# A hybrid encoder layer: one pair of work tiles kept at another address, and five small reorderings in its first stage

## The chip, the cores and the metric

The kernel runs on one core of one Trainium2 chip. The metric is the device time of one execution in microseconds (us). The engines are named as in the profile: PE is the matrix engine (PEld its weight loads), DVE the vector engine, ACT the scalar engine, POOL the engine that also takes small element-wise work, SP the queue from which most transfers are issued. Each engine works through its own instructions in a fixed order and waits on semaphores for the others.

## The reference, cut to what matters

Two sequences of 1024 rows by 1024 columns go through one encoder layer. The part that the change touches is the input side of the mixing sub-layer:

```
h = rmsnorm(x, g_mix) * (1.0 + sc1) + sh1          # sc1, sh1 from silu(c) @ w_ada
z = h @ w_in                                        # 256 + 128 + 64 + 512 columns
q_lat, kv_lat, k_pe, f_in = split(z)
y_mla  = attention(rmsnorm(q_lat), rmsnorm(kv_lat), rope(k_pe))
y_four = real(fft2(f_in over sequence and group columns)) @ w_four
mix = concat([y_mla, y_four]) @ w_out
x = x + ga1 * mix
```

Behind it stand a gated feed-forward layer (2816 wide) and a final norm. All results are float32.

## The kernel before

**Stages.** Stage 1 (from 0 to about 223 us) makes the latents and the Fourier inputs. Stage 2 (to about 300 us) does the transform along the sequence, multiplies it into the folded output weights and makes the second modulation. Stage 3 is attention (to about 680 us), and the feed-forward part fills the rest. Nearly every product is made of three matmuls on float32 operands that are split in a high and a low half: `split` writes the high half on ACT (line 62) and the low half on DVE (line 63), and `mm3` issues the three matmuls (lines 83 to 85).

**Stage 1** runs over eight pairs k = 0 to 7, four for each sequence. A pair is two blocks of 128 rows, j and j + 4, which the Fourier part adds and subtracts. For each pair there are these steps, and the steps of neighbouring pairs overlap:

- `norm_sq`: squares of the rows on ACT (line 377), then `rstd`, a chain of six small instructions on POOL (lines 107 to 114, from `rs_v` to `rs_r`). `norm_x`: the rows `xt` scaled by `rs_r` on DVE (line 389).
- `flip`: 16 transposes on PE (line 405) in two pairs of groups, g = 0, 1 and g = 2, 3, into PSUM banks; ACT and DVE read them out to `hf`, `hh` and `hl`.
- `zproj` / `z_mm`: the latent columns of z on PE. `z_out`: their squares on ACT (lines 462 and 463), `rstd` on POOL again (`rs_v<-mz`), the rotary key on DVE and POOL (lines 480 to 484) and the normalised latents `lat` on DVE (lines 486 and 487).
- `latents`: four transposes of `lat` for each of the two blocks on PE (line 501), split by ACT into `lh` and by DVE into `ll`, and two stores to `lat_d` in HBM.
- `evenodd`: sums and differences `eo` of the two blocks on POOL (line 428), split by ACT into `eoh` and by DVE into `eol`. There is one `eo` buffer.
- `fourier_in(k, 0)` and `fourier_in(k, 1)`: 24 matmuls each with 280 and 256 columns, called the cosine and the sine product below.

Between these steps a generator, `extras()`, is called for one step at a time by `next(more)`. It makes the modulation row (matmuls at line 219, transfers of `wada`), `fold_q` (eight matmuls at line 242, results taken out of PSUM by DVE at line 243), `fold_out` and last the folding of the output gate into `wm_d`: four matmuls at line 325 and four results `so` on DVE (line 330) for each step, which leave by stores to HBM. `so`, `lat` and the modulation row share three buffers (tag `sk`).

**What sets the order.** The program is written in one order and put into an order for each engine when it is built; `issue_after(x)`, `chained(f)` (behind the last named PE instruction) and `behind()` (behind the last split) constrain that order. On the chip the order of each engine is fixed, and an instruction that waits holds up all that stand behind it on its engine.

**Memory.** The tiles of stage 1 lie in a pool `p1`. Stage 2 opens pools over the same addresses, with waits for each tile: a tile of stage 2 may be written when the tiles of stage 1 that lay there are done with. In the kernel before, the two buffers each of `lh` and `ll` lie at bytes 91424 to 99616 of a partition, and three stage 2 tiles lie on them: the small `An` and `nyn`, `ny` (93984) and `A` (from 96032). `ny` is written by line 899, `A` by the first splits of stage 2.

## Time and profile before

| what | value |
|---|---|
| median of 3 runs | 2037.05 us (2036.78 to 2038.44) |
| the profiled execution: its own time / its span | 2039.17 us / 2037.4 us |
| mean granted PE clock | 0.993 |
| PE busy over the span | 1988.9 us, 98% |
| PE busy 0 to 223 us | 206.5 of 223 us |
| PE busy 223 to 300 us | 74.7 of 77 us |
| PE busy 300 to 680 us | 373.8 of 380 us |
| PE busy 680 to 2037 us | 1333.9 of 1357 us |

The profile shows one execution, which took 2.1 us more than the median of the runs; 1.77 us of its time lie outside the span. A timeline row reads: start, busy time (both in us), engine, line of the kernel, operation, result and operands, number of instructions, and in brackets the idle time of the engine ahead of the row with what ended it. The windows view gives for a stretch the busy time of each engine, then the clock granted to PE (1.00 is full speed, 0.50 half), then the share of the transfer engines that was busy.

### The profile page before, as it was taken

To read this page: it belongs to the slowest core of one execution; us is meant where nothing else is said; L and a number is where in the kernel's file an instruction comes from. 1 tells how busy PE (TensorE), PEld (TensorE's weight loads), DVE (VectorE), ACT (ScalarE), POOL (GpSimd) and SP (SyncE) were. 2 spreads that over 40 slices of the span, in tenths; PEclk is the share of its full clock that TensorE was granted. 3 is DMA by queue.
4 is the path that set the end of the run, shared out by engine and by line. 5 is a ranking of instruction groups with operands and counts; after the bars stand their busy time and mean duration, and the time that the engine had idled before them with its cause. 6 is when DMAs were issued, how large, how long until landed. Compare 5 with 4: busy or idle time off the path is not lost.

```text
span 2037.4 us, 28290 instructions
## 1 busy us (share of the span) xinstructions
PE 1988.9 (98%) x9840; PEld 1624.8 (80%) x9840; DVE 1415.8 (69%) x2088; ACT 896.8 (44%) x1733; POOL 828.6 (41%) x1013
## 2 busy tenths in 40 slices
PE   8899999999999999999999999999999999999997
PEld 7688777888777778888888888877788888888876
DVE  5676657766676679888677677677756655657674
ACT  4565545555555564333333365453333333336441
POOL 2454112111313227879779410333654454510142
PEclk9999999999999999999999999999999999999999
DMA  9685793445554475545645587674422322357662
GB/s 377 209 289 169 235 346 116 114 104 120 144 125 134 120 265 195 197 169 193 210 160 193 177 301 252 217 234 148 138 98 104 113 95 103 114 189 269 229 217 90
DMA packets 181963, 370.33 MB, mean 182 GB/s; under 512 B 18556, under 2 KB 58236, under 8 KB 177724
## 3 DMA queue, kind: packets, MB, share of 16 engines
q1 hardware_dynamic: 163148, 310.71, 45.5%
q0 software_dynamic: 18672, 57.81, 9.3%
q8 instruction: 77, 1.26, 0.3%
q14 instruction: 66, 0.54, 0.1%
HBM read 256.46 MB, written 120.39 MB: 185 GB/s over the span
## 4 chain that ended last, share of the span: by engine, by line
PE 54%; DVE 2%; DMA 2%; POOL 1%; issue 1%; ACT 1%; SPq 0%; DVEq 0%; ACTq 0%; POOLq 0%
PE bank L84 18%; PE bank L83 18%; PE bank L85 18%; DVE wl L63 1%; DMA val<-x_d 1%; DMA draw<-s_d 1%; DVE val L143 1%; POOL val L143 0%; ACT wh L62 0%; DVE val L1761 0%; DMA draw<-t_d 0%; POOL rs_y L110 0%; DVE val L1735 0%; DMA rgu<-in_wgu_dram 0%; DMA draw<-in_w_down_dram 0%
## 5 line engine op out<-in xcount | busy, mean ns | idle before, releaser
L83 PE MATMUL bank<-H,wh 128*128 128x512 f32 x1224 | 477.2, 390 | 6.4 <-DVE val L143 5.8
L85 PE MATMUL bank<-H,wl 128*128 128x512 f32 x1224 | 476.4, 389 | 0.2 <-DVE wl L63 0.2
L84 PE MATMUL bank<-H,wh 128*128 128x512 f32 x1224 | 476.2, 389 | 0.0
L143 DVE TENSOR_TENSOR val<-bank,val 128x512 f32<-128x512 f32 x244 | 166.7, 688 | 164.7 <-PE bank L85 163.5
L83 PEld LDWEIGHTS bank<-H,wh 128*128 128x128 f32 x1224 | 229.7, 188 | 56.9 <-DVE val L143 6.6
L85 PEld LDWEIGHTS bank<-H,wl 128*128 128x128 f32 x1224 | 229.7, 188 | 49.1 <-DVE wl L63 1.5
L84 PEld LDWEIGHTS bank<-H,wh 128*128 128x128 f32 x1224 | 229.7, 188 | 47.6
L63 DVE TENSOR_TENSOR wl<-draw,wh 128x512 fp32r<-128x512 f32 x286 | 201.6, 740 | 83.5 <-ACT wh L62 83.0
L62 ACT CAST wh<-draw 128x512 fp32r<-128x512 f32 x286 | 168.9, 621 | 158.9 <-PE bank L84 81.5
L84 PE MATMUL bank<-wl,wh 128*128 128x512 f32 x572 | 223.6, 391 | 3.5 <-DVE wl L63 3.5
L143 POOL TENSOR_TENSOR val<-val 128x512 f32<-128x512 f32 x58 | 82.7, 1434 | 347.4 <-DVE val L1735 192.4
L83 PE MATMUL bank<-wh 128*128 128x512 f32 x572 | 222.7, 389 | 0.4 <-ACT wh L62 0.4
L85 PE MATMUL bank<-wh,wl 128*128 128x512 f32 x572 | 222.6, 389 | 0.0
L62 ACT CAST wh<-rgu 128x512 fp32r<-128x512 f32 x171 | 106.5, 624 | 250.4 <-PE bank L84 194.1
L63 DVE TENSOR_TENSOR wl<-val,wh 128x512 fp32r<-128x512 f32 x133 | 142.9, 1076 | 70.6 <-ACT wh L62 70.5
L63 DVE TENSOR_TENSOR wl<-rgu,wh 128x512 fp32r<-128x512 f32 x171 | 166.7, 976 | 7.6 <-ACT wh L62 7.5
L62 ACT CAST wh<-val 128x512 fp32r<-128x512 f32 x133 | 82.4, 623 | 178.7 <-PE bank L84 158.3
L140 POOL TENSOR_TENSOR val<-rgu 128x512 f32<-128x512 f32 x80 | 114.1, 1426 | 99.7 <-DMA rgu<-in_wgu_dram 91.0
L84 PEld LDWEIGHTS bank<-wl,wh 128*128 128x128 f32 x572 | 107.3, 188 | 28.7 <-DVE wl L63 6.6
L83 PEld LDWEIGHTS bank<-wh 128*128 128x128 f32 x572 | 107.4, 188 | 23.2 <-ACT wh L62 0.8
L85 PEld LDWEIGHTS bank<-wh,wl 128*128 128x128 f32 x572 | 107.4, 188 | 22.1
L140 POOL TENSOR_TENSOR val<-val 128x512 f32<-128x512 f32 x89 | 119.3, 1357 | 1.3
(393 smaller groups left out, 3924.2 us busy)
## 6 DMA issues: line engine op xcount, KB each, us to landing
rgu<-in_wgu_dram SPq DMA_DIRECT2D x86, 512.0 KB, 4.9
draw<-s_d SPq DMA_DIRECT2D x143, 256.0 KB, 3.8
s_d<-val POOLq DMA_DIRECT2D x88, 256.0 KB, 3.9
draw<-t_d SPq DMA_DIRECT2D x88, 256.0 KB, 4.1
s_d<-val SPq DMA_DIRECT2D x66, 256.0 KB, 3.5
wada<-in_wa_dram SPq DMA_DIRECT2D x16, 1024.0 KB, 11.8
draw<-in_w_down_dram SPq DMA_DIRECT2D x55, 256.0 KB, 4.5
xt<-in_x_dram SPq DMA_DIRECT2D x16, 512.0 KB, 6.9
```

The source lines that it names most:

```text
L62: here["a"] = nc.scalar.copy(hi, src).ins
L63: here["v"] = nc.vector.tensor_tensor(out=lo, in0=src, in1=rd(hi), op=ALU.subtract).ins
L83: nc.tensor.matmul(out, lh, rh, start=first, stop=False, skip_group_check=cont)
L84: nc.tensor.matmul(out, lh, rl, start=False, stop=False, skip_group_check=cont)
L85: here["pe"] = nc.tensor.matmul(out, ll, rh, start=False, stop=last, skip_group_check=cont).ins
L140: return eng.tensor_tensor(out=out, in0=x, in1=y, op=ALU.subtract).ins
L143: return eng.tensor_tensor(out=out, in0=x, in1=y, op=ALU.add).ins
```

## The change

Five edits, all in stage 1:

1. Two dummy tiles for each of the tags `lh` and `ll` are taken right behind the Fourier weights of pool `p1`. A tag keeps its place, so `lh` and `ll` lie at bytes 83136 to 91328, and `ropec`, `ropes`, `c2`, `lw`, `zoc`, `vecs`, `scT` and `b1` move up by 8192 bytes. The stage 2 tiles `An`, `ny` and `A` stay where they are and now lie on some of these. No instruction is added.
2. `fold_q` issues both matmuls of a head, and then both DVE operations.
3. `z_out(0)` (the squares of pair 0's latents and what follows) is placed ahead of `norm_sq(2)`, which is held behind its last square.
4. In pairs 5 and 6 the first of the three `extras()` steps is left out at its place and called at the end of the pair.
5. In the last pair the latents of its second block are flipped behind the sine product; before, behind the cosine product.

```diff
--- before.py
+++ after.py
@@ -192,6 +192,9 @@
         wz_l = w.tile([P, NC, DZ], F32R, name="wz_l")
         wcs_f = [w.tile([P, NC * NCS + NZC - NCOS], F32R, name=f"wcs_{x}") for x in "hl"]
         wcs_h, wcs_l = [t[:, : NC * NCS].rearrange("p (c n) -> p c n", c=NC) for t in wcs_f]
+        for t in ("lh", "ll"):
+            for _ in range(2):
+                w.tile([P, 512], F32R, tag=t, name=t, bufs=2)
         ropec = w.tile([P, 8, ROPE], F32, name="ropec")
         ropes = w.tile([P, 8, ROPE], F32, name="ropes")
         c2 = w.tile([P, P], F32, tag="c2", name="c2")
@@ -240,6 +243,7 @@
             ps = bank()[:, : 2 * P].rearrange("p (a b) -> p a b", a=2)
             for c in range(2):
                 here["pe"] = nc.tensor.matmul(ps[:, c, :], wuqT[:, h, c * P : (c + 1) * P], wukT[:, h, :], start=True, stop=True).ins
+            for c in range(2):
                 nc.vector.scalar_tensor_tensor(
                     out=wq[:, c, h * P : (h + 1) * P], in0=ps[:, c, :], scalar=gq[:, c : c + 1], in1=gkvr,
                     op0=ALU.mult, op1=ALU.mult)
@@ -683,8 +687,9 @@
             chained(flip_t, 1, g)
             flip_s(1, g)
         with behind():
+            z_out(0, range(2), pz)
+        with tc.issue_after(here["sq"]):
             norm_sq(2)
-            z_out(0, range(2), pz)
         norm_x(2)
 
         def pair(k, also=None):
@@ -713,7 +718,8 @@
             if k < nk - 1:
                 flip(k + 1, 0)
                 flip(k + 1, 1)
-            next(more, None)
+            if k < 5:
+                next(more, None)
             if k > 1:
                 zproj(k, 1)
             if 1 < k < nk - 1:
@@ -727,15 +733,20 @@
             fourier_in(k, 0)
             if k in (1, nk - 1):
                 chained(latents, k, 0)
+            if k == 1:
                 chained(latents, k, 1)
-            else:
+            elif k < nk - 1:
                 latents(k, 1)
             if k + 1 < nk:
                 evenodd(k + 1, 0)
             next(more, None)
             fourier_in(k, 1)
+            if k == nk - 1:
+                chained(latents, k, 1)
             if k + 1 < nk:
                 evenodd(k + 1, 1)
+            if k >= 5:
+                next(more, None)
 
         for k in range(1, nk - 1):
             pair(k)
```

No engine gets an instruction more or fewer. How the built order moves is shown at three places. `bank` is a PSUM bank; line numbers of the changed kernel are 3 or 4 higher.

**POOL, end of pair 0 and start of pair 1**; before, from the end of the chain for the rows of pair 2 (`ms`) to the sums and differences of pair 1:

```order
L114 TENSOR_TENSOR rs_r<-rs_w,rs_y 128x2
L484 TENSOR_TENSOR lat<-t_757 128x64 x2
L107 TENSOR_SCALAR rs_v<-mz 128x4
L110 TENSOR_TENSOR rs_y<-rs_v,mhalf 128x4
L111 TENSOR_TENSOR rs_w<-rs_y 128x4
L112 TENSOR_TENSOR rs_w<-rs_w,rs_v 128x4
L113 TENSOR_SCALAR rs_w<-rs_w 128x4
L114 TENSOR_TENSOR rs_r<-rs_w,rs_y 128x4
L484 TENSOR_TENSOR lat<-t_771 128x64 x2
L428 TENSOR_TENSOR eo<-hf 128x512 x4
```

and now:

```order
L114 TENSOR_TENSOR rs_r<-rs_w,rs_y 128x4
L488 TENSOR_TENSOR lat<-t_760 128x64 x2
L432 TENSOR_TENSOR eo<-hf 128x512 x2
L107 TENSOR_SCALAR rs_v<-ms 128x2
L110 TENSOR_TENSOR rs_y<-rs_v,mhalf 128x2
L111 TENSOR_TENSOR rs_w<-rs_y 128x2
L112 TENSOR_TENSOR rs_w<-rs_w,rs_v 128x2
L113 TENSOR_SCALAR rs_w<-rs_w 128x2
L114 TENSOR_TENSOR rs_r<-rs_w,rs_y 128x2
L432 TENSOR_TENSOR eo<-hf 128x512 x2
```

The chain for the rows of pair 2 stood ahead of that for the latents of pair 0 (`mz`). Now it stands behind it, and between the first two and the last two `eo` of pair 1.

**DVE, the same place**; before, from the first scaling of pair 2's rows:

```order
L389 TENSOR_SCALAR xt<-xt,rs_r 128x1024
L63 TENSOR_TENSOR kv<-lat,kv 128x128
L389 TENSOR_SCALAR xt<-xt,rs_r 128x1024
L63 TENSOR_TENSOR eol<-eo,eoh 128x512 x2
L63 TENSOR_TENSOR ll<-bank,lh 128x512 x2
L63 TENSOR_TENSOR eol<-eo,eoh 128x512 x2
L480 TENSOR_TENSOR t_898<-bank,ropec 128x64
```

and now:

```order
L63 TENSOR_TENSOR kv<-lat,kv 128x128 x2
L393 TENSOR_SCALAR xt<-xt,rs_r 128x1024 x2
L63 TENSOR_TENSOR eol<-eo,eoh 128x512 x4
L63 TENSOR_TENSOR ll<-bank,lh 128x512 x2
L484 TENSOR_TENSOR t_902<-bank,ropec 128x64
```

The two `ll` of pair 0 stood between the `eol` of sums and of differences; now all four `eol` stand ahead of them. On ACT `lh` moves in the same way behind four `eoh`.

**PE, the last pair**; before, from the end of the cosine product into the sine product:

```order
L84 MATMUL bank<-wcs_l,eoh 128x280
L85 MATMUL bank<-wcs_h,eol 128x280
L501 MATMUL bank<-ident,lat 128x128 x8
L83 MATMUL bank<-wcs_h,eoh 128x256
L84 MATMUL bank<-wcs_l,eoh 128x256
L85 MATMUL bank<-wcs_h,eol 128x256
```

and now the same place and, behind the mark, the end of the sine product with the first matmuls of stage 2:

```order
L84 MATMUL bank<-wcs_l,eoh 128x280
L85 MATMUL bank<-wcs_h,eol 128x280
L505 MATMUL bank<-ident,lat 128x128 x4
L83 MATMUL bank<-wcs_h,eoh 128x256
L84 MATMUL bank<-wcs_l,eoh 128x256
...
L85 MATMUL bank<-wcs_h,eol 128x256
L505 MATMUL bank<-ident,lat 128x128 x4
L83 MATMUL bank<-tb_2618,zh_2602 128x258
L84 MATMUL bank<-tb_2619,zh_2602 128x258
```

Four of the eight transposes of `lat` move behind the 24 matmuls of the sine product, straight ahead of stage 2. In pair 5 the four matmuls of line 325 that stood ahead of the second `zproj` and the four behind the flips 2 and 3 become four behind these flips and four behind the latents, ahead of the sine product.

## The prediction

> **What bounds the kernel now.** The page's first part comes first: PE is busy for all but 48.5 us of the span of 2037.4 us.
>
> ```profile
> PE 1988.9 (98%) x9840; PEld 1624.8 (80%) x9840; DVE 1415.8 (69%) x2088; ACT 896.8 (44%) x1733; POOL 828.6 (41%) x1013
> ```
>
> The change adds no PE work, so only two things can move the end: idle time of PE, and time in which PE runs at half clock. All edits lie in the first 300 us. Of PE's waits there I take those beside the edited steps from its timeline: first pairs 0 and 1, then pair 5, then the last pair and the entry of stage 2.
>
> ```profile
> 67.93 0.30 PE L405 MATMUL bank<-ident,xt 128*128 128x128 f32 x1 [1.03 <-DVE xt L389]
> 68.86 0.98 PE L405 MATMUL bank<-ident,xt 128*128 128x128 f32 x7 [0.64 <-DVE xt L389]
> ...
> 70.67 1.25 PE L405 MATMUL bank<-ident,xt 128*128 128x128 f32 x8 [0.60 <-DVE ll L63]
> 74.70 0.80 PE L242 MATMUL bank<-wukT,zraw 128*128 128x128 f32 x2 [2.78 <-DVE zraw L243]
> ...
> 77.75 0.58 PE L83 MATMUL bank<-wcs_h,eoh 128*128 128x280 f32 x1
> ...
> 183.44 0.41 PE L501 MATMUL bank<-ident,lat 128*128 128x128 f32 x2 [1.86 <-DVE lat L486]
> ...
> 219.80 0.63 PE L501 MATMUL bank<-ident,lat 128*128 128x128 f32 x4 [1.14 <-DVE lat L486]
> ...
> 229.22 0.38 PE L84 MATMUL bank<-tb,zh 128*128 128x256 f32 x1 [1.75 <-DVE tb L63]
> 230.16 0.45 PE L85 MATMUL bank<-tb,zn 128*48 128x258 f32 x1 [0.55 <-DVE zn L63]
> ```
>
> The windows view shows the clock around them. The second number is PE's busy time, the last three are PEclk, the busy share of the transfer engines and GB/s.
>
> ```profile
> 66.30:69.70 3.40, 1.73 (x17) 0.98 (x10) 3.01 (x6) 2.07 (x6) 0.67 (x1) 1.00 0.26 77
> 69.70:73.10 3.40, 1.62 (x12) 1.01 (x10) 2.50 (x4) 1.03 (x2) 2.50 (x2) 1.00 0.59 181
> 73.10:76.50 3.40, 1.79 (x10) 0.71 (x10) 2.18 (x10) 3.40 (x14) 1.80 (x4) 0.50 1.01 296
> 76.50:79.90 3.40, 3.40 (x18) 2.60 (x12) 2.17 (x6) 1.69 (x4) 2.65 (x8) 0.50 0.43 164
> 79.90:83.40 3.50, 3.50 (x29) 2.52 (x28) 3.33 (x8) 3.47 (x8) 1.20 (x1) 0.99 0.30 79
> ...
> 226.70:230.10 3.40, 1.15 (x8) 0.75 (x6) 2.03 (x7) 1.17 (x4) 0.00 (x0) 1.00 0.33 84
> 231.00:232.00 1.00, 1.00 (x7) 0.92 (x6) 0.86 (x5) 0.41 (x4) 0.00 (x0) 0.50 1.01 291
> ```
>
> Half clock comes in stretches of 3.4 us: two from 73.1 to 79.9, and one behind 230.1. Stretches with 1.15 or 1.62 us of PE work in 3.4 (34%, 48%) were followed by half clock, one with 1.73 (51%) was not; 1.79 us inside a slow stretch did not end it, 3.40 us did. A fully busy slow stretch does half its work, so it costs 1.7 us on top of the gap that brought it on.
>
> The Trainium skill, "TensorE: Matmul & The Clock Gate", Part 1, "What's actually happening", has the gate watch a free-running window of some 3.4 us and close after an idle one. The length agrees with the stretches above; the idle window does not, since here gaps of 1.75 and 2.78 us were enough. By that rule the gap at 229 us would cost its idle time alone, and the gain forecast below would be 1.7 us smaller (2035.1 us).
>
> **The last pair and stage 2 (edits 1 and 5).** These rows show who held DVE, ACT and then SP:
>
> ```profile
> 228.07 0.43 DVE L899 TENSOR_SCALAR ny<-raw 128x512 fp32r<-128x512 f32 x1 [3.90 <-DMA lat_d<-lh]
> ...
> 228.48 1.28 DVE L63 TENSOR_TENSOR tb<-raw,tb 128x512 fp32r<-128x512 f32 x2
> ...
> 220.15 1.07 ACT L62 CAST lh<-bank 128x512 fp32r<-128x512 f32 x2
> ...
> 228.93 1.20 ACT L62 CAST A<-bank 128x256 fp32r<-128x256 f32 x4 [6.33 <-DMA lat_d<-ll]
> ...
> 224.65 1.39 SPq L1039 DMA_DIRECT2D scT<-sc_d  x1
> 228.60 0.33 SPq L985 DMA_DIRECT2D wraw<-wm_d  x1
> ...
> 231.33 0.43 SPq L1058 DMA_DIRECT2D wada<-in_w_ada_dram x1
> ```
>
> `ny` and `A` lie on `lh` and `ll`, whose last stores land at about 228; the two `tb` and `zn`, for which PE waits, stand behind `ny`. At the new address of `lh` and `ll` the tiles under `ny` and `A` were last read earlier in stage 1, so nothing but the order of the engines holds them. With edit 5 PE goes from the cosine into the sine product without the 1.14 us. The second `lat`, there just before 219.80, is flipped behind the sine product at 221.5; its `lh` ends at 222.6, its `ll` at 223.5, `ny` at 224.1 and the two `tb` (1.28) at 225.4. PE wants them at 228.1 less the gap of 1.75 and less 1.14, about 226: some 0.7 us to spare. Gone are 1.14, 1.75 and 0.55 us of idle time and the slow stretch behind, 1.70: 5.14 us.
>
> What lies behind is now wanted earlier:
>
> ```profile
> 238.83 0.75 DVE L999 SCALAR_TENSOR_TENSOR wn<-wnh,cmask,wnr 128x512 fp32r<-128x512 f32 x1
> ...
> 239.81 0.61 PE L1011 MATMUL bank<-wn,ny 128*128 128x512 f32 x2
> ...
> 269.76 0.16 PEld L1051 LDWEIGHTS bank<-wada,scT 128*32 128x32 f32 x8 [0.46 <-DMA wada<-in_w_ada_dram]
> ...
> 250.00:260.00 10.00, 10.00 (x53) 5.59 (x55) 2.61 (x5) 1.64 (x3) 0.00 (x0) 1.00 1.01 347
> ```
>
> `wn` is ready 0.2 us ahead of the matmul that reads it, behind a queue on ACT and DVE that moves up a little less than PE; I take a wait of 0.4 us. The chunks of the second modulation are the harder limit: the transfer engines are full from 250 to 260 us (1.01), and chunk 6 came just as PE wanted it (0.46). SP issues the first chunk 2.73 us behind its first read of `wm_d`, which waited for `ny` and `nyn` to free a buffer. `ny` is 4 us earlier, but SP now has the last two stores to `lat_d` until about 224.5 and `scT` (1.39) behind them, so the read goes at 225.9 and the chunk at 228.6, 2.7 us earlier. PE asks for it 4.7 us earlier. Between no wait at all (0) and all that exceeds 2.7 us (2.0) I take 1.1, the middle, since chunks are held in four buffers. Left: 5.14 - 0.4 - 1.1 = **3.6 us**, bounds 2.0 (with waits of 3.1 in all) and 5.1.
>
> **Pair 5 (edit 4).** The transposes at 183.44 wait for `lat`, the last of a queue on DVE:
>
> ```profile
> 178.86 1.28 DVE L330 TENSOR_TENSOR so<-bank,gah 128x512 f32<-128x512 f32 x2
> ...
> 182.82 0.47 DVE L486 TENSOR_SCALAR lat<-bank,rs_r 128x256 f32<-128x256 f32 x1
> ```
>
> Three `so` stood in that queue (these two and a third, 0.64 each) and, with their stores, in the three buffers that `lat` shares with them. All come behind `lat` now, so the wait of **1.86 us** goes. What moved, four matmuls of line 325, four `so` and their stores on SP, has the sine product and pair 6 as its cover, where PE waits for nothing. Without that cover `lat(6,0)` would be late by its buffer; the stores leave by about 190 and it is written at about 195, so 5 us are to spare. Bounds 0 and 1.86.
>
> **Pairs 0 and 1 (edits 2 and 3).** Here I expect a loss. The rows of ACT, POOL and DVE:
>
> ```profile
> 56.30 1.05 ACT L377 ACTIVATE junk<-xt 128x1024 bf16<-128x1024 f32 x1
> 58.66 0.39 ACT L462 ACTIVATE junk<-bank 128x256 bf16<-128x256 f32 x1
> ...
> 58.72 0.22 POOL L107 TENSOR_SCALAR rs_v<-ms 128x2 f32<-128x2 f32 x1 [10.40 <-ACT junk L377]
> 60.65 0.20 POOL L114 TENSOR_TENSOR rs_r<-rs_w,rs_y 128x2 f32<-128x2 f32 x1
> 61.48 0.23 POOL L107 TENSOR_SCALAR rs_v<-mz 128x4 f32<-128x4 f32 x1
> 64.47 2.50 POOL L428 TENSOR_TENSOR eo<-hf 128x512 f32<-128x512 f32 x2
> 70.16 2.50 POOL L428 TENSOR_TENSOR eo<-hf 128x512 f32<-128x512 f32 x2 [3.19 <-DVE eol L63]
> ...
> 67.04 0.74 DVE L389 TENSOR_SCALAR xt<-xt,rs_r 128x1024 f32<-128x1024 f32 x1
> 69.92 1.28 DVE L63 TENSOR_TENSOR ll<-bank,lh 128x512 fp32r<-128x512 f32 x2
> ```
>
> Pair 0's squares start at 56.3 instead of 58.66, so the sums `eo` run from 61.4 to 63.9 instead of from 64.47. The chain for pair 2's rows (2.1 us, 58.72 to 60.85) now follows them and ends at 66.0; `xt` starts there, 1.0 us earlier than before, and the first flips gain that. But DVE's first two `eol` stand behind `xt` and end at 68.7, and POOL's differences, in the one `eo` buffer, behind these: 68.8 to 71.3. ACT casts them until 72.0 and only then `lh`; DVE has their `eol` until 72.7, then the first `ll` until 73.3. PE's second flips need the banks that `ll` frees. They had them at 70.67 and now get them at 73.35, with PE out of work from 69.6: one gap of 3.7 us where 0.60 and 2.78 stood. So the 2.78 us that edit 2 removes come back as a wait for `ll`. Pair 1's squares follow `lh` (73.0 to 74.5), its chain with the two additions of `lat` between takes 3.1 us, and the cosine product's bank is now the one that `lat(1,0)` frees at 78.4: it starts at 78.5 instead of 77.75, 0.7 us lost. PE is idle from 75.7 until then, so the stretch from 76.5 has 43% of work and the clock should stay at half until 83.35: 1.7 us lost; four of eight `fold_q` matmuls that stood inside slow or full stretches are done ahead, 0.5 us back. Sum **-1.9 us**. Bounds: -3.0, with one more late bank of 1.1 us as at 67.93; above, +2.8 if the wait is simply gone, and +5 with the slow stretches gone too. I stay near the lower end, since each step of it is a fixed order and a duration from a row.
>
> **Sum.** 3.6 + 1.9 - 1.9 = 3.6 us. The profiled 2039.17 us becomes 2035.6; the median of the runs before stood 2.12 us under that execution, so 2037.05 - 3.6 gives **2033.4 us**. Behind 300 us the order is the same; a gap there may fall otherwise on the 3.4 us stretches, 1.7 us each, either way.
>
> **Rivals.** (a) *Pairs 0 and 1 gain too*: banks come early enough, or the clock stays up, +1 to +3 there, and stage 2 keeps its 5.1: 8 to 10 us, **2028 us**. For it, every named wait vanishes; against it, `ll` behind four `eol`. (b) *Most is handed back*: stage 2 keeps 2.0, pairs 0 and 1 lose 3.0, pair 5 gives 1.9: 0.9 us, **2036 us**. For it, the full transfers and the chunk that came just in time. That edit 1 does nothing, since `ny` would wait for another late tile, comes to nearly the same: 1.14 + 1.86 - 1.9, 1.1 us. (c) *Slower*: the later `ll` and `lat` push pair 1, and the flips' read-out on ACT and DVE then trails PE, so that z of each further pair waits for `hl`. A gap as at 229 with its slow stretch is 3.4 us a pair; from the third pair on it outweighs the 5.5 us of the other places: 10.2 - 5.5, **2042 us**. Against it, PE waits for nothing between 85 and 183 us, so 0.7 us of delay find slack.
>
> **How the numbers follow.** Forecast 0.52, (a) 0.22, (b) 0.20, (c) 0.06. A difference under 0.2% (4.07 us) cannot be told from none. The forecast's own range is 2031 to 2036, and 0.44 of it lies beyond 4.07 us: faster 0.23 + 0.22 = 0.45, same 0.29 + 0.20 = 0.49, slower 0.06. The range 2029.0 to 2037.5 takes in (b) and the nearer part of (a), and leaves (c) out.
>
> **What would show it.** Right: PE without idle time ahead of the `tb` matmuls and PEclk 1.00 from 226 to 234; no wait for `lat` in pair 5; a gap of 3 to 4 us ahead of flips 2 and 3 of pair 2, ended by `ll`, and PEclk 0.50 past 80 us. Wrong: `ny` still behind a transfer; those flips within 1 us of the first ones; a new wait for `wada` of over 2 us.

## The result, and the profile after

| | before | changed |
|---|---|---|
| median of 20 runs each | 2037.09 us | 2033.77 us |
| ratio, with its 95% interval | 1 | 0.9983 (0.9976 to 0.9990) |
| the profiled execution: its own time / its span | 2039.17 / 2037.4 us | 2032.84 / 2031.1 us |

The changed kernel is 0.17% faster, 3.3 us between the medians, against a forecast of 2033.4 us. One of the 20 runs of each kernel took over 2469 us (the changed kernel's at a granted clock of 0.75), and the ratio is that of the other 19. By the 0.2% of the prediction the gain falls on the side of "cannot be told from none", though its interval does not reach 1. The two profiled executions differ by 6.3 us; 2.4 of these come from a place that no edit touches, as shown below.

The page's first part of the changed kernel has PE busy 3.4 us less, with the same instructions. Idle time fell from 48.5 to 45.6 us.

```profile
PE 1985.5 (98%) x9840; PEld 1621.9 (80%) x9840; DVE 1405.3 (69%) x2088; ACT 896.3 (44%) x1733; POOL 824.3 (41%) x1013
```

With the same work, less busy time means that PE ran less of it at half clock. In the clock records, before had half-clock stretches at 73.1 (6.8 us long), 230.1, 325.7 and 650.0 us (3.4 us each). The changed kernel has two, at 73.4 and 643.4 us (3.4 us each). Both have those at the program's two ends too.

PE's timeline of the changed kernel at the edited places:

```profile
73.49 1.97 PE L409 MATMUL bank<-ident,xt 128*128 128x128 f32 x8 [3.33 <-DVE ll L63]
...
78.29 0.40 PE L83 MATMUL bank<-wcs_h,eoh 128*128 128x280 f32 x1 [1.62 <-DVE lat L491]
...
195.70 0.44 PE L505 MATMUL bank<-ident,lat 128*128 128x128 f32 x2 [1.09 <-DVE lat L490]
...
240.46 1.07 PE L1062 MATMUL bank<-wada,scT 128*32 128x512 f32 x8 [1.83 <-DMA wada<-in_w_ada_dram]
...
271.65 0.38 PE L83 MATMUL bank<-tb,zh 128*128 128x256 f32 x1 [1.08 <-DVE ed L143]
...
321.41 1.06 PE L1226 MATMUL ppt<-ident,p 128*128 128x128 f32 x8 [1.21 <-DVE nb L1208]
```

The waits for `zraw`, for `lat` in pair 5 (1.86) and for `tb` and `zn` (1.75, 0.55) are gone. Others are new or grown: 3.33 for `ll` and 1.62 for `lat` in pair 1, 1.09 for `lat` of pair 6, 1.83 for a chunk `wada` (a piece of the weights of the second modulation), and 1.08 in the middle of stage 2, where the second sequence begins (`tb` behind `ed`).

The windows view of the changed kernel shows the clock at pairs 0 and 1 and at the entry of stage 2:

```profile
69.97:73.38 3.41, 0.19 (x4) 0.00 (x0) 2.33 (x4) 2.51 (x7) 1.49 (x2) 1.00 0.00 0
73.39:76.80 3.41, 3.17 (x12) 2.49 (x12) 1.39 (x8) 2.93 (x11) 2.00 (x6) 0.50 0.88 243
76.81:80.20 3.39, 1.91 (x14) 1.92 (x15) 2.71 (x7) 1.94 (x6) 2.20 (x6) 1.00 0.99 303
223.00:240.00 17.00, 15.56 (x91) 11.96 (x89) 13.34 (x34) 13.72 (x33) 0.53 (x1) 1.00 0.99 324
226.00:230.00 4.00, 4.00 (x27) 3.44 (x27) 3.77 (x9) 3.88 (x10) 0.00 (x0) 1.00 0.96 297
230.00:234.00 4.00, 4.00 (x19) 3.00 (x17) 3.67 (x6) 2.98 (x6) 0.53 (x1) 1.00 0.91 322
```

PE is fully busy at full clock from 226 to 234 us, where before had 1.15 of 3.4 us and then half clock. The half-clock stretch at 73.4 ends after one length, 3.17 of its 3.41 us being busy; the stretch behind it, with 1.91 busy, stays at full clock.

**Where the time went.** For the same matmul of PE, counted from the first, its start in the changed kernel less its start in before says how much has been gained so far (us; marks by the start in before; worked out from the two traces, at marks where both kernels have issued the same matmuls):

| mark in before | place | shift so far | the step of the prediction | measured there |
|---|---|---|---|---|
| 94.1 | pairs 0 and 1 | -0.5 | +1.9 | -0.5 |
| 202.8 | pair 5, start of pair 6 | -1.7 | -1.86 | -1.2 |
| 247.9 | last pair, entry of stage 2, first chunks | -5.2 | -3.6 | -3.5 |
| 283.7 | second sequence of stage 2 | -3.9 | none | +1.3 |
| 322.9 | start of attention | -3.7 | none | +0.2 |
| 363.4 | attention | -6.1 | either way | -2.4 |
| 2026.7 | end | -6.3 | none | -0.2 |

By the mark at 283.7 the change gains 3.9 us in this pair of executions, and the forecast was 3.6. But three of its parts are off by 2.4, 0.7 and 1.3 us, and these cancel. The experiments take the parts one by one.

### The profile page after: what moved, and what is told of

It is laid out like the page before. It is cut to its first block, busy times and chain, and to the rows that moved or that the text cites. A ratio compares the mean times of both kernels' runs of the same rounds, so it can differ in the third digit from the quotient of the medians.

```text
span 2031.1 us, 28284 instructions
## 1 busy us (share of the span) xinstructions
PE 1985.5 (98%) x9840; PEld 1621.9 (80%) x9840; DVE 1405.3 (69%) x2088; ACT 896.3 (44%) x1733; POOL 824.3 (41%) x1013
## 4 chain that ended last, share of the span: by engine, by line
PE 51%; DMA 3%; DVE 3%; issue 1%; POOL 1%; ACT 1%; SPq 1%; DVEq 0%; ACTq 0%; POOLq 0%
PE bank L84 17%; PE bank L83 17%; PE bank L85 17%; DVE wl L63 1%; DMA val<-x_d 1%; DMA H<-s_d 1%; ACT wh L62 1%; DMA draw<-s_d 1%; POOL val L143 1%; DVE val L143 1%; DMA draw<-t_d 0%; DVE val L1772 0%; SPq L1732 0%; SPq L1731 0%; POOL rs_y L110 0%
## 5 line engine op out<-in xcount | busy, mean ns | idle before, releaser
L83 PEld LDWEIGHTS bank<-H,wh 128*128 128x128 f32 x1224 | 229.8, 188 | 56.7 <-DVE val L143 7.1
L85 PEld LDWEIGHTS bank<-H,wl 128*128 128x128 f32 x1224 | 229.8, 188 | 49.4 <-DVE wl L63 1.5
L84 PEld LDWEIGHTS bank<-H,wh 128*128 128x128 f32 x1224 | 229.8, 188 | 47.3
L63 DVE TENSOR_TENSOR wl<-val,wh 128x512 fp32r<-128x512 f32 x133 | 134.1, 1010 | 74.4 <-ACT wh L62 74.4
```

Source lines behind the costliest of these rows:

```text
L63: here["v"] = nc.vector.tensor_tensor(out=lo, in0=src, in1=rd(hi), op=ALU.subtract).ins
L83: nc.tensor.matmul(out, lh, rh, start=first, stop=False, skip_group_check=cont)
L84: nc.tensor.matmul(out, lh, rl, start=False, stop=False, skip_group_check=cont)
L85: here["pe"] = nc.tensor.matmul(out, ll, rh, start=False, stop=last, skip_group_check=cont).ins
```

## The experiments

Each kernel's time stands beside runs of before on the same chip. The table gives the ratio with its 95% interval and the shift against before's profiled execution, worked out as above. Each shift compares one execution with one execution of before, which took 2.1 us more than the median given above, so times are judged by the ratio and places by the rows. The last column lists the half-clock stretches from 60 to 700 us (start, and length where it is not 3.4).

| kernel | us (before) | ratio | 94.1 | 202.8 | 283.7 | 322.9 | 363.4 | half clock at |
|---|---|---|---|---|---|---|---|---|
| edit 1 alone | 2032.26 (2035.17) | 0.9981 (0.9972 to 0.9991) | +0.3 | +0.2 | -2.8 | -2.2 | -3.3 | 76.6, 646.6 |
| edit 5 alone | 2038.04 (2035.17) | 1.0010 (1.0002 to 1.0019) | +0.3 | +2.6 | +2.9 | +2.8 | +3.2 | 76.7, 185.9, 329.3, 653.5 |
| edits 1 and 5 | 2033.16 (2035.17) | 0.9990 (0.9981 to 0.9999) | +0.6 | +0.6 | -2.1 | -1.7 | -1.5 | 69.8, 76.6, 325.8 |
| edit 4 alone | 2033.06 (2035.17) | 0.9990 (0.9981 to 1.0000) | +0.4 | -0.3 | -2.8 | -3.2 | -3.0 | 70.3 (10.2), 322.9, 647.1 |
| edit 2 alone | 2036.55 (2036.93) | 1.0003 (0.9994 to 1.0012) | -1.2 | -1.2 | -0.7 | -0.5 | -0.3 | 76.2, 229.8, 325.4, 649.7 |
| edit 3 alone | 2037.93 (2036.93) | 1.0007 (0.9998 to 1.0016) | +2.6 | +2.4 | +0.6 | +0.8 | -1.5 | 71.5 (10.2), 648.4 |
| changed, without edit 3 | 2032.72 (2036.93) | 0.9984 (0.9976 to 0.9993) | -1.2 | -1.5 | -4.4 | -4.1 | -4.3 | 76.0, 321.7, 646.0 |
| changed, first `ll` ahead | 2033.24 (2036.93) | 0.9983 (0.9974 to 0.9992) | -1.4 | -2.5 | -5.4 | -5.3 | -5.1 | 72.4 (6.8), 321.6 |
| changed, chunks later | 2030.45 (2036.79) | 0.9970 (0.9957 to 0.9982) | +1.0 | -0.2 | -4.8 | -5.3 | -7.7 | 71.9 (10.2), 641.9 |
| changed, pair 1 in another order | 2029.56 (2036.79) | 0.9960 (0.9947 to 0.9974) | -3.2 | -4.4 | -7.1 | -7.2 | -8.2 | none |
| both of these | 2026.42 (2036.79) | 0.9944 (0.9932 to 0.9956) | -2.3 | -3.1 | -7.8 | -7.4 | -9.8 | 75.2 |
| both, without edit 5 | 2027.23 (2037.03) | 0.9953 (0.9941 to 0.9965) | -1.9 | -3.1 | -7.3 | -8.0 | -7.6 | 73.1 (6.8), 318.8 |

### Edit 1 alone: `lh` and `ll` at another address

```diff
+        for t in ("lh", "ll"):
+            for _ in range(2):
+                w.tile([P, 512], F32R, tag=t, name=t, bufs=2)
         ropec = w.tile([P, 8, ROPE], F32, name="ropec")
```

> Kernel before with edit 1 alone (lh and ll at the new address). Theory (ny and A waited only for the last stores to lat_d, because they lie on lh and ll): PE's gaps of 1.75 and 0.55 us ahead of the tb and zn matmuls are gone and PEclk is 1.00 from 226 to 234, while the 1.14 us wait for lat in the last pair stays. Gross 4.0 us; a wait for the first wada chunk takes back 1 to 2.5 of it, since the transfer engines are full there. Net 1.5 to 3 us by 280 us. Rival (ny also waits for something else, or the gain needs edit 5): a gap of over 1 us ahead of tb stays, net under 0.5 us.

PE's timeline of this kernel, its one wait from 222 to 270 us:

```profile
242.88 1.06 PE L1054 MATMUL bank<-wada,scT 128*32 128x512 f32 x8 [1.18 <-DMA wada<-in_w_ada_dram]
```

DVE's timeline, `ny` and the two `tb`:

```profile
224.28 0.42 DVE L902 TENSOR_SCALAR ny<-raw 128x512 fp32r<-128x512 f32 x1
...
224.69 1.29 DVE L63 TENSOR_TENSOR tb<-raw,tb 128x512 fp32r<-128x512 f32 x2
```

`ny` starts at 224.28 without a wait, where before it started at 228.07 behind 3.90 us for a store of `lh`. The gap at `tb` and its half-clock stretch are gone, and 1.18 us of it come back at a chunk. On PE, DVE, ACT and POOL all instructions come in the same order as in before, so nothing but the address differs. Edit 1 gives 3.0 us between the marks 202.8 and 283.7, and in time as much as all five edits together (0.9981 and 0.9983).

### Edit 5 alone: the last flip behind the sine product

```diff
             if k in (1, nk - 1):
                 chained(latents, k, 0)
+            if k == 1:
                 chained(latents, k, 1)
-            else:
+            elif k < nk - 1:
                 latents(k, 1)
...
             fourier_in(k, 1)
+            if k == nk - 1:
+                chained(latents, k, 1)
```

> Kernel before with edit 5 alone (second latents of the last pair flipped behind the sine product). Theory: the 1.14 us wait goes, but ny still waits for the store of the second ll, which does not land earlier than before; PE comes 1.1 us earlier to tb and waits there for 2.5 to 3.5 us in all. Net -0.5 to +0.5 us at 236 us. Rival (edit 5 is worth its 1.14 us by itself): gap at tb as before, net +1.1 us.

PE's timeline of this kernel at the same place, and one row of DVE's:

```profile
225.91 0.39 PE L83 MATMUL bank<-tb,zh 128*128 128x258 f32 x1 [0.44 <-DVE ll L63]
...
231.34 0.38 PE L84 MATMUL bank<-tb,zh 128*128 128x256 f32 x1 [2.19 <-DVE tb L63]
...
278.34 0.38 PE L83 MATMUL bank<-tb,zh 128*128 128x256 f32 x1 [1.08 <-DVE ed L143]
```

```profile
230.19 0.43 DVE L902 TENSOR_SCALAR ny<-raw 128x512 fp32r<-128x512 f32 x1 [4.34 <-DMA lat_d<-lh]
```

The 1.14 us in the last pair are gone, and 0.44 at `ll` and 0.44 more at `tb` (2.19 for 1.75) come, since `ny` still waits for the later stores. Before's half-clock stretch at 230.1 is missing here, so by 238 us the kernel has still gained 1.9 us since 202.8; a wait of 0.82 us for a chunk and one of 1.08 at the second sequence take that back. From 202.8 to 283.7 it loses 0.3 us. The 2.2 us that it lost between the marks 94.1 and 202.8 lie ahead of its edit; a half-clock stretch at 185.9, which no other kernel has, stands there. The profiled execution is the slowest of the eleven (2040.62 us), and the median too is 0.1% slower than before, which these rows do not explain. Edit 5 alone gains nothing.

### Edits 1 and 5 together

> Kernel before with edits 1 and 5 (no edit at pairs 0, 1, 5 and 6). Theory: as in the changed kernel, no gap at tb and no 1.14 us wait, 5.1 us gross at 236 us, 1.5 to 2.5 us handed back as one wait for the first wada chunk: net 2.6 to 3.6 us. Then these two edits are the greater part of the change's gain of 3.3 us. Rival (the change's gain comes from pairs 0, 1 and 5): net under 1.5 us.

PE's timeline of this kernel:

```profile
224.18 0.39 PE L83 MATMUL bank<-tb,zh 128*128 128x258 f32 x1 [0.64 <-DVE ll L63]
...
273.39 0.39 PE L83 MATMUL bank<-tb,zh 128*128 128x256 f32 x1 [1.08 <-DVE ed L143]
```

From 202.8 to 283.7 the two give 2.7 us, edit 1 alone gave 3.0. Of the 1.1 us that edit 5 takes out of the last pair, 0.64 return at the entry of stage 2 and 1.08 at its second sequence. That last wait stands in all six kernels that have edit 5 and the chunks at their old place, and in none of those without edit 5. Edit 5 changes two things there. One is which PSUM bank each later product gets, since `bank()` hands them out in a ring and the four transposes now draw theirs later. The other is the built order behind the edit: against before, PE's differs at places from 230 to 240, 264 to 265 and 277 to 279 us, and DVE's and ACT's at places from 273 to 294 us (times of before). The wait is put down to `ed`, which DVE reads out of a bank; that the ring of banks is the cause and not the order is argued, and no run separates the two.

### Edit 4 alone: the folding steps of pairs 5 and 6

```diff
-            next(more, None)
+            if k < 5:
+                next(more, None)
...
                 evenodd(k + 1, 1)
+            if k >= 5:
+                next(more, None)
```

> Kernel before with edit 4 alone (folding steps of pairs 5 and 6 later). Theory of the forecast: the 1.86 us wait for lat in pair 5 goes and nothing takes its place: 1.9 us by 200 us. Rival, as the trace of the changed kernel suggests: a wait of about 1.1 us for lat of pair 6 takes its place, because the moved so stand ahead of it on DVE: 0.8 us by 200 us. Whether it reaches stage 2's end depends on the stores to lat_d there: they move with it, so the same number by 240 us in both.

PE's timeline of this kernel; the wait of 1.86 us in pair 5 is gone:

```profile
197.04 0.44 PE L501 MATMUL bank<-ident,lat 128*128 128x128 f32 x2 [1.35 <-DVE lat L486]
...
227.30 0.39 PE L84 MATMUL bank<-tb,zh 128*128 128x256 f32 x1 [1.06 <-DVE tb L63]
```

The first row is new and gives most of it back: 0.7 us are left between 94.1 and 202.8, as the rival had it. DVE's timeline of the changed kernel shows why, with POOL's row beside it:

```profile
193.04 0.69 DVE L334 TENSOR_TENSOR so<-bank,gah 128x512 f32<-128x512 f32 x1
193.64 1.61 DVE L63 TENSOR_TENSOR hl<-hf,hh 128x512 fp32r<-128x512 f32 x1
195.17 0.47 DVE L490 TENSOR_SCALAR lat<-bank,rs_r 128x256 f32<-128x256 f32 x1
...
193.41 1.29 POOL L432 TENSOR_TENSOR eo<-hf 128x512 f32<-128x512 f32 x1
```

In before the two `hl` of this place stood behind `lat`; now a moved `so` and both `hl` stand ahead of it, and the second `hl` takes 1.61 us instead of 0.69 beside POOL's `eo`.

The second row is a surprise: the wait for `tb` is 1.06 instead of 1.75, though nothing there is edited, the order behind 203 us is that of before, and no half-clock stretch follows. So 2.4 of the 2.8 us that this kernel gains by 283.7 come behind 202.8, from a gap that edit 1 closes anyway; the two gains don't add. The wait is shorter because `ny` waited 2.93 us for the store of `lh` and not 3.90. Edit 3 alone, which touches nothing there either, has 3.12 for `ny` and 0.96 for `tb`; edit 2 alone has 4.03 and 1.88. So at the old address the price of this wait differs by about 1 us from kernel to kernel, and a half-clock stretch follows it in two of these four (before and edit 2 alone). With one profile of each, it is open what makes the store late, and the 3.0 us of edit 1 are measured against one of the dearer cases.

### Edits 2 and 3, each alone, and the changed kernel without edit 3

```diff
                 here["pe"] = nc.tensor.matmul(...).ins
+            for c in range(2):
                 nc.vector.scalar_tensor_tensor(
```

> Kernel before with edit 2 alone (both fold_q matmuls, then both DVE operations). Theory: the wait of 2.78 us for zraw was that of a second matmul on one bank; without it PE goes on to the flips and the cosine product, which is then held only by the bank it takes over. The order of POOL, ACT and DVE (ll between the two pairs of eol) is as before, so flips 2 and 3 of pair 2 come at 70.5 to 71 and the cosine product of pair 1 at 75 to 78.5, up to 2.7 us earlier than the 77.75 of before. Rival (the cosine product waits for lat of pair 1 anyway, ready at 78.4): it starts at 78.3 to 78.6, no gain.

```diff
         with behind():
-            norm_sq(2)
             z_out(0, range(2), pz)
+        with tc.issue_after(here["sq"]):
+            norm_sq(2)
```

> Kernel before with edit 3 alone (squares of pair 0 ahead). Theory: it is this edit that puts ll behind four eol on DVE and lh behind four eoh on ACT: flips 2 and 3 of pair 2 wait for ll until 73.3 to 73.6 after a gap of 3 to 4 us, and the cosine product of pair 1 starts no earlier than before. Loss 0.5 to 2 us by 95 us. Rival (the earlier squares are a gain by themselves): cosine product before 77 us.

The third kernel is the changed one with the second of these diffs undone.

> Changed kernel without edit 3. Theory (edit 3 costs at pairs 0 and 1, the rest gains): place of pairs 0 and 1 as with edit 2 alone, so 0 to 2.7 us faster than the changed kernel by 95 us; behind it as the changed kernel: 2031 to 2034 us median. Rival (edit 3 is needed for edit 2 to gain): 0.5 to 2 us slower than the changed kernel.

PE's timelines at pairs 0 and 1: edit 2 alone, then edit 3 alone, then the changed kernel without edit 3.

```profile
75.48 0.71 PE L242 MATMUL bank<-wukT,zraw 128*128 128x128 f32 x4 [3.23 <-ACT hf L418]
```

```profile
73.44 1.97 PE L405 MATMUL bank<-ident,xt 128*128 128x128 f32 x8 [4.53 <-DVE ll L63]
...
78.24 0.60 PE L83 MATMUL bank<-wcs_h,eoh 128*128 128x280 f32 x1 [2.05 <-DVE lat L487]
```

```profile
75.33 0.71 PE L245 MATMUL bank<-wukT,zraw 128*128 128x128 f32 x4 [3.23 <-ACT hf L421]
```

Edit 2 takes the wait for `zraw` away and finds ACT's read-out `hf` late at the same point; the gap keeps its place and its releaser changes (2.78, now 3.23). At 94.1 this kernel is 1.2 us ahead, with one half-clock stretch where before has two, and its time is that of before (1.0003). Edit 3 makes the gap that the prediction walked out, at 73.4, ended by `ll`; alone it is 2.6 us behind at 94.1, more than expected. By the traces edit 3 costs something in the changed kernel too (-1.2 without it, -0.5 with it at 94.1), but the times of the changed kernel with and without it, 0.9983 and 0.9984, don't tell them apart.

### The first `ll` ahead of the differences of pair 1

If the gap at 73.5 is there because `ll` stands behind four `eol`, it should close when `ll` is put ahead of the last two. The same edit puts the chain for pair 2's rows ahead of the sums on POOL:

```diff
-                with tc.issue_after(here["rope"]):
+                ms2 = here["p"]
+                with tc.issue_after(ms2):
                     evenodd(1, 0)
                 for u in range(2):
                     chained(latents, 0, u)
-                with tc.issue_after(here["rope"]):
+                with behind():
                     evenodd(1, 1)
-                with behind():
                     z_out(1, range(2), pz1)
```

> Changed kernel in which the chain for pair 2's rows stands ahead of the sums of pair 1 on POOL, and the lh and ll of pair 0 stand ahead of the differences' eoh and eol on ACT and DVE. Theory (the 3.33 us gap is head-of-line: ll behind four eol, which stand behind xt): the gap ahead of flips 2 and 3 goes, these start by 69 to 70 us; the cosine product of pair 1 then waits for lat of pair 1 (chain behind all sums and differences) and starts at 73 to 75 instead of 78.3 us. Gain 3 to 5 us over the changed kernel by 95 us. Rival (the flips wait for another bank, or the differences come too late for the sine product): the gap moves, gain under 1 us.

PE's timeline of this kernel:

```profile
73.19 1.22 PE L245 MATMUL bank<-wukT,zraw 128*128 128x128 f32 x4 [3.16 <-ACT hf L421]
...
76.17 0.60 PE L83 MATMUL bank<-wcs_h,eoh 128*128 128x280 f32 x1 [1.76 <-DVE lat L491]
```

The second flips now run at 68.9 without a wait, and the gap moves behind them, to `hf`: 3.16 for 3.33 us. The rival was right that closing this gap opens another one. The cosine product starts at 76.17, 2.1 us earlier than in the changed kernel and later than expected. At 94.1 only 0.9 us are left of these, and the time is the same (0.9983).

### The chunks of the second modulation one step later

The changed kernel's wait of 1.83 us for a chunk should go when each chunk is asked for one step of stage 2 later:

```diff
-                    if n > 0:
-                        mod2(n - 1)
+                    if n > 1:
+                        mod2(n - 2)
                     if n == 7:
+                        mod2(6)
                         mod2(7)
```

> Changed kernel in which stage 2 takes each of the first modulation chunks one step later (the first behind the third of the eight output products instead of the second, the last two together at the end). Theory (the 1.83 us wait at 240 us is for a chunk that cannot land earlier, because the transfer engines are full, and PE has other work there): the wait goes, the other chunks have landed when they are used, 1.5 to 2 us faster than the changed kernel by 282 us. Rival (stage 2 is bound by its transfers): the wait comes back at a later chunk, under 0.5 us.

PE's timeline of this kernel, its one wait from 223 to 300 us:

```profile
276.38 0.66 PE L151 MATMUL bank<-ident,modrow 128*128 128x128 f32 x4 [1.04 <-DVE modrow L1102]
```

The wait for the chunk is gone, and so is the wait at the second sequence; 1.04 us come back at the read-out of the modulation row. From 202.8 to 283.7 this kernel gains 4.6 us against 2.2 of the changed one, and the time is 2030.45 us, 0.9970.

Its order at pairs 0 and 1 is that of the changed kernel, instruction for instruction. The windows view of it there:

```profile
71.90:75.30 3.40, 1.97 (x9) 1.58 (x9) 2.64 (x9) 3.37 (x14) 0.81 (x2) 0.50 0.47 132
75.30:78.70 3.40, 1.78 (x7) 1.49 (x7) 1.37 (x5) 1.49 (x4) 2.30 (x9) 0.50 1.04 280
78.70:82.10 3.40, 3.40 (x17) 3.40 (x16) 3.40 (x8) 3.40 (x9) 2.02 (x2) 0.50 1.02 320
```

Three half-clock stretches, where the changed kernel had one; at 94.1 the shift is +1.0 instead of -0.5. The waits are the same to 0.01 us (3.33 and 1.62). The only difference that the rows show is where the 3.4 us stretches begin: at 71.9 here, so that 1.97 of 3.40 us are busy and the clock stays down, and at 73.4 in the changed kernel, so that 3.17 are busy and it comes back.

### Pair 1 in another order, and both together

POOL here does the chain for pair 2's rows, the sums, the chain for pair 1's latents, and then the differences; the latents of pair 1 stand behind the first `ll` on DVE, and the squares of pair 3 behind the differences. Its core:

```diff
-                with tc.issue_after(here["rope"]):
+                ms2 = here["p"]
+                mz1 = tiny.tile([P, 4], F32, name="mz")
+                for u in range(2):
+                    z_sq(pz1[u], mz1[:, 2 * u : 2 * u + 2])
+                with tc.issue_after(ms2):
                     evenodd(1, 0)
+                rz1 = rstd(mz1, 4)
...
-                with tc.issue_after(here["rope"]):
-                    evenodd(1, 1)
-                with behind():
-                    z_out(1, range(2), pz1)
...
+            if k == 1:
+                with tc.issue_after(ll0), tc.issue_after(here["a"]):
+                    for u in range(2):
+                        z_rest(1, u, pz1[u], rz1[:, 2 * u : 2 * u + 2])
+                with behind(), tc.issue_after(p1):
+                    evenodd(1, 1)
...
```

> Changed kernel with another order at pairs 0 and 1: on POOL pair 2's rows, the sums, pair 1's latents, the differences; on ACT lh and the read-out of flips 0 and 1 of pair 2 ahead of kv of pair 1 and of the differences; on DVE ll ahead of the differences. Theory (place is bound by head-of-line waits on POOL, ACT and DVE, not by their work): flips 2 and 3 of pair 2 at 68 to 70 us with under 1 us of wait, cosine product of pair 1 at 70 to 72 instead of 78.3 us, no or one stretch of half clock: 6 to 9 us faster than the changed kernel by 95 us, and most of it kept by 200 us. Rival (the transfers of stage 1, with their engines 0.86 busy from 95 to 160 us, or the read-out of the flips, take over): half of it or more comes back as waits for wada, xt or hl before 200 us.

Rows of PE's, ACT's and POOL's timelines of this kernel:

```profile
73.85 0.71 PE L245 MATMUL bank<-wukT,zraw 128*128 128x128 f32 x4 [3.56 <-ACT hf L421]
74.32 0.38 PE L83 MATMUL bank<-wcs_h,eoh 128*128 128x280 f32 x1
...
84.90 1.06 PE L222 MATMUL bank<-wada,scT 128*32 128x512 f32 x8 [1.31 <-DMA wada<-in_wa_dram]
...
72.78 1.47 ACT L421 ACTIVATE hf<-bank,sh1b,s1b 128x256 f32<-128x256 f32 x3 [4.30 <-POOL eo L432]
...
70.26 2.48 POOL L432 TENSOR_TENSOR eo<-hf 128x512 f32<-128x512 f32 x2
```

The wait of the cosine product for `lat` is gone; it starts at 74.32 instead of 78.29. It was expected at 70 to 72: one gap of 3.56 us stays, and here its cause is plain. `hf` has one buffer, POOL's differences of pair 1 read it until 72.74, and ACT starts to write pair 2's into it at 72.78. A wait of 1.31 us for a transfer at 84.9 is new, as the rival had it. At 94.1 this kernel has gained 3.2 us, 2.7 more than the changed kernel where 6 to 9 were expected, and the time is 0.9960.

> The two changes of the runs before together. Theory: their gains add, 7 to 10 us faster than the changed kernel, a median of 2024 to 2027 us where the kernel before has 2037. Rival (the first chunk of stage 2 comes still later relative to PE, which is earlier): a wait of over 2 us for wada in stage 2, gain 4 to 6 us.

With the later chunks as well it takes 2026.42 us, ratio 0.9944: faster than before by 0.56%, where the changed kernel is by 0.17%. PE's timeline of it shows two waits that are still to be had:

```profile
194.23 0.44 PE L505 MATMUL bank<-ident,lat 128*128 128x128 f32 x2 [1.09 <-DVE lat L490]
...
273.33 0.66 PE L151 MATMUL bank<-ident,modrow 128*128 128x128 f32 x4 [1.04 <-DVE modrow L1115]
```

> The kernel with both the new order at pairs 0 and 1 and the later chunks, but without edit 5 (second latents of the last pair behind the cosine product again). Theory (edit 5 gives back what it gains, because one bank of PSUM is taken later and the ring of banks has shifted by one: waits of 0.4 to 0.6 us for ll and of 1.08 us at the start of the second sequence): the 1.1 us wait for lat in the last pair is back, and the wait of 1.04 us in the second sequence's first steps is gone; within 0.5 us of the kernel with edit 5 at 282 us, median within 2 us of 2026.4. Rival (edit 5 is a gain of its own 1.1 us once the address is changed): 1.1 us or more slower at 282 us.

This is the last kernel with edit 5 undone, the diff of edit 5 read backwards. PE's timeline:

```profile
216.05 0.63 PE L505 MATMUL bank<-ident,lat 128*128 128x128 f32 x4 [0.51 <-DVE lat L490]
...
273.88 0.66 PE L151 MATMUL bank<-ident,modrow 128*128 128x128 f32 x4 [1.04 <-DVE modrow L1112]
```

The wait of the last pair comes back at 0.51 us, and from 202.8 to 283.7 the gain is 4.1 us instead of 4.7. So with the chunks out of the way edit 5 is worth about 0.5 us in the trace; the times, 0.9944 and 0.9953, overlap in their intervals. The wait for `modrow` stays at 1.04: it belongs to the later chunks and not, as expected, to edit 5.

## Why the prediction was right, point by point

**The sum.** 2033.4 us was forecast and 2033.77 measured; within 0.2% was given the largest chance, 0.49, and the ratio is 0.9983. The reasons are right in kind at two of three places, but the closeness of the sum is luck: pairs 0 and 1 came out 2.4 us better, pair 5 with the start of pair 6 about 0.7 worse, and the second sequence of stage 2 1.3 worse.

**The last pair and stage 2: right.** Step by step: `ny` is held by the address alone (edit 1 alone shows it), the gap at `tb` and its half-clock stretch go, and the transfers give part back. The term of 3.6 us measured 3.5. Two of its parts were off. The wait of 0.4 us for `wn` did not come. The wait for a chunk was 1.83 us and not 1.1, within the bounds of 0 and 2.0, and it was the second chunk and not the first. SP's rows in the changed kernel:

```profile
227.21 0.43 SPq L1069 DMA_DIRECT2D wada<-in_w_ada_dram  x1
...
231.18 0.52 SPq L1069 DMA_DIRECT2D wada<-in_w_ada_dram  x1
```

The first chunk was issued at 227.21, where 228.6 was forecast, and was there when PE came to it at 234.4. The second was issued at 231.18 and PE had it at 240.46. In before it was issued at 238.12 and used at 245.66 without a wait:

```profile
238.12 0.38 SPq L1058 DMA_DIRECT2D wada<-in_w_ada_dram  x1
...
245.66 1.07 PE L1051 MATMUL bank<-wada,scT 128*32 128x512 f32 x8
```

So the second chunk's issue had moved by 6.9 us, as much as PE, and it is the transfer that had become longer. By the trace's records of landings it was complete at 240.42 in the changed kernel, 9.2 us after its issue, and at 243.75 in before, 5.6 us after it. In before the first chunk had landed at 237.83, ahead of that issue; in the changed kernel it landed at 234.34, 3.2 us behind it, so the two shared the transfer engines. These were 0.98 busy while the second was under way, and 0.90 in before. Over the whole entry of stage 2, from 223 to 240 us, they were 0.99 busy, and in before 0.79:

```profile
223.00:240.00 17.00, 14.68 (x89) 13.17 (x88) 11.30 (x30) 9.87 (x27) 0.37 (x1) 0.90 0.79 244
```

The prediction worked the wait out from the issue; what set it is how long the chunk was under way beside the others. The 3.1 us of waits in the prediction's lower bound are not summed from rows; 1.83 came here. And the gain was booked to edits 1 and 5 together, though edit 5 gave nothing on top of edit 1: beside edit 1 it takes away 1.09 us in the last pair and 0.53 at the chunk, and 0.64 at `ll` and 1.08 at the second sequence come. It is worth about 0.5 us in the one place where the chunks are later.

**The second sequence of stage 2: missed.** The step "what lies behind is now wanted earlier" looked at transfers and `wn` alone. A wait of 1.08 us for `tb` behind `ed` at 271.65 comes with edit 5, by a path that no row of before shows.

**Pair 5: the cover was named wrongly.** The 1.86 us went as forecast. "The sine product and pair 6 as its cover, where PE waits for nothing" failed: the step asked when `lat(6,0)` gets its buffer, and that was early enough, but on DVE a moved `so` and two `hl` now stand ahead of it. That costs 1.09 us here and 1.35 alone.

**Pairs 0 and 1: the walk was right, the clock was not.** The walk through POOL, DVE and ACT had the sums at 61.4, the chain's end at 66.0, the differences at 68.8, PE's second flips at 73.35 and the cosine product at 78.5. The rows of the changed kernel:

```profile
61.41 2.59 POOL L432 TENSOR_TENSOR eo<-hf 128x512 f32<-128x512 f32 x2
...
66.03 0.20 POOL L114 TENSOR_TENSOR rs_r<-rs_w,rs_y 128x2 f32<-128x2 f32 x1
68.95 2.50 POOL L432 TENSOR_TENSOR eo<-hf 128x512 f32<-128x512 f32 x2 [2.73 <-DVE eol L63]
```

With PE's 73.49 and 78.29 each is met within 0.25 us. The failed step is "the clock should stay at half until 83.35: 1.7 us lost", and with it the reading that PE would idle from 75.7: flips and `fold_q` ran at half clock and lasted until 76.67, so that their stretch was 93% busy and the clock came back. The kernel with the later chunks shows that the forecast was one of two outcomes of the same order: there the clock stays down until 82.1 and the shift is +1.0 instead of -0.5. Within an execution the stretches lie on one grid: the four of before at 73.1, 230.1, 325.7 and 650.0 are 46, 28 and 95 times 3.413 us apart. In the fourteen profiled executions it lies at different offsets from the start, so the term should have been a range of at least 1.5 us, not a value. The sign "PEclk 0.50 past 80 us" failed with it; the other signs came.

**The rivals.** (a) was refuted where it mattered: a gap of over 3 us stands in pairs 0 and 1 in the changed kernel and in every kernel with edit 2 or 3, and stage 2 did not keep its 5.1. That one slow stretch fewer came goes back to the phase of this grid, as the kernel with the later chunks shows. (b) had the right suspect, the transfers, and too much of it. (c) did not happen: no wait of a further pair for `hl` appears.

**What stays open.** The 2.4 us between 322.9 and 363.4. The row that stands there in the changed kernel is the wait for `nb` of 1.21 us at 321.41; before had this one:

```profile
326.43 1.94 PE L1215 MATMUL ppt<-ident,p 128*128 128x128 f32 x8 [2.54 <-DVE nb L1197]
```

That wait was 1.2 to 1.3 us in the four kernels that gain 2.3 to 2.4 us there (the changed one, edit 3 alone, the later chunks, and these with the new order of pair 1), and 2.1 to 2.7 in the others, most of them with a half-clock stretch right there. What sets the one or the other was not tried. All four have edit 3, but so do three of the others; the order of the four engines behind 300 us is the same in all kernels; and edit 3 alone shows the gain in its profile and is not faster in its time. So the 2.4 us cannot be credited to an edit, nor is chance shown.

## What to carry to other kernels

When a tile of a later stage waits for the last store of an earlier one, look first at what lies on its address: moving a pair of tiles added no instruction and gave as much as the whole change, while the four reorderings of the change mostly renamed their waits. Before crediting a removed wait, walk each engine's queue past the moved instruction for everything that now stands ahead of something, not only for buffers, and see what full transfers do to it. And a term for the half clock should be a range: in these runs a drop needed a gap, but where the gap lay on the 3.4 us grid went into whether it came and how long it lasted.

## What the runs showed of the hardware

**The phase of the clock gate.** The same instructions with the same waits met one half-clock stretch or three (changed kernel, later chunks), for 1.5 us between them at 94.1. Five kernels with before's order at pairs 0 and 1 (before, edits 1, 5, 1 and 5, 4) had two, one, one, two (not adjoining) and three, and yet lie within 0.6 us of each other at 94.1; so the number of stretches alone is not the price. In the rows here a half-clock stretch with 3.17 of 3.41 us busy ended it, and ones with 1.97 and 1.78 did not. The prediction's reading of the way down, between 48% and 51% of work, is no sharp limit: in edit 1 alone a stretch of the grid with 1.60 of 3.41 us busy (47%, from 322.4) was followed by full clock, and in edit 4 alone one with 1.75 (51%, from 66.9) by half. The Trainium skill, "TensorE: Matmul & The Clock Gate", Part 1, "What's actually happening", calls the window free-running and its effect different from run to run; these runs agree, with one stretch against three. It has that for the start of a kernel and advises not to fit to it; here it acts in mid-kernel, and 1.5 us are nearly half of the change's whole gain.

**DVE beside POOL.** Scaling the rows `xt` took DVE 1.42 us for two when POOL was idle (changed kernel), and 3.44 when POOL's sums started just ahead of it (first `ll` ahead), where POOL's two took 2.96 instead of 2.50:

```profile
66.26 1.42 DVE L393 TENSOR_SCALAR xt<-xt,rs_r 128x1024 f32<-128x1024 f32 x2 [2.11 <-POOL rs_r L114]
```

```profile
63.09 3.44 DVE L393 TENSOR_SCALAR xt<-xt,rs_r 128x1024 f32<-128x1024 f32 x2 [0.72 <-POOL rs_r L114]
...
63.01 2.96 POOL L432 TENSOR_TENSOR eo<-hf 128x512 f32<-128x512 f32 x2
```

The 1.61 us of `hl` in pair 6 look alike: POOL's `eo` had started 0.23 us ahead of it. The Trainium skill, "SBUF — State Buffer", "Who interferes with whom", has the two engines share a pair of ports, which for some forms of DVE's instructions the one that comes first holds for a whole instruction; the rows agree, as each `xt` takes 1.0 us more, which is less than one of POOL's instructions (1.25). So a reordering that lets POOL start earlier can make a DVE step beside it more than twice as long, which no row of before need show.
